# One shared pool of four PSUM banks for scores, transpositions and value products

## The chip, the cores and the metric

The kernel runs on one core of one Trainium2 chip. The metric is the device time of one execution in microseconds (us). The runs shown of the kernel before took 1342.78, 1343.08 and 1343.51 us; their median is 1343.08 us.

## The reference, cut to what matters

Two decoder layers over 512 tokens of width 1024: a recurrent layer (RG-LRU and SSD mixers), a SwiGLU FFN, a layer of dilated sliding-window attention with 16 heads of 64, and a second FFN. The change touches the attention layer, and the recurrent layer through the same pool of banks.

```python
s = jnp.einsum('bnqhe,bnkhe->bnhqk', qb, kc)
s = jnp.where(valid[None, :, None], s, -jnp.inf)
m = jnp.max(s, axis=-1)
p = jnp.exp(s - m[..., None])
o = jnp.einsum('bnhqk,bnkhe->bnqhe', p, vc)
```

The three (window, dilation) patterns are merged by their denominators. The kernel does that with one mask: it adds the logarithm of how many patterns allow a pair of tokens to its score, and takes a single softmax.

## The kernel before, in words

Everything stands transposed (channels on partitions, tokens along the free side). Each large product is made of three matmuls of split operands (high times high and the two mixed terms); the weights are loaded by SP, their high part is made by ACT and their low part by DVE (POOL for the attention's weights), line 107. PE is fed by these.

PSUM has eight banks, and a tile of 128 x 512 float32 fills one. Pool `pa` has four (tag `pa`: the projections, lines 234, 302, 735, 876). Pool `pm` has three under tag `pm` (`bufs=3`, line 77) and a fourth under tag `po` (line 848), which only the value product uses. Tag `pm` serves the sums of the norms (lines 212, 222), the recurrent layer (lines 319 to 554) and, in the attention:

- `pair_T(p)` (line 783): two tiles, the transposed queries and keys of a pair of heads; ACT and DVE copy them out as `qk_hi` and `qk_lo`.
- `scores(p)` (line 812): for both heads of a pair and three blocks b = 0, 1, 2 of query tiles, one tile per head (six tiles, called s0a, s0b, s1a, s1b, s2a, s2b below). DVE reads each piece once (line 833, mask and row minimum), ACT takes the exponential (line 834), DVE the reciprocal (line 837), POOL multiplies by it (line 839).
- `values(h)` (line 841): for each of three groups of key tiles, PE transposes the probabilities into a `pm` tile (line 855; 4, 4 and 2 transpositions), ACT and DVE split it (`ph`, `pl`, lines 91 and 92), and PE multiplies with the values into the one tile `ps_o` (lines 863, 864). Then ACT copies half of `ps_o` (line 866) and DVE adds the halves (line 867).

`attend(half)` (line 890) writes down: `pair_T` and `scores` of the next pair, then `values` of both heads of this one. The heads come in two halves of four pairs. The three parts of `qkv_part(1, ...)`, the projections of the second half, stand in the text behind the whole of `attend(0)`, and the output projection `out_proj(0, ...)` is called between the values of `attend(1)`.

The text isn't the order in which an engine works. When the kernel is built, the framework writes each engine's queue with a planner of its own: an instruction whose inputs are ready may be put ahead of earlier text, and a tile gets a bank of its tag when one comes free. On the chip each queue then runs in the order written, each instruction waiting for the semaphores of those it needs.

Of the kernel before, what the change touches and what calls it, by code (L numbers as in the profile page):

```python
# [10 lines left out]
F32 = mybir.dt.float32  # L11
# [6 lines left out]
P = 128  # L18
D = 1024
T = 512  # L20
# [39 lines left out]
def trunk(ctx: ExitStack, tc: tile.TileContext, a):  # L60
# [13 lines left out]
    ss_ = ctx.enter_context(tc.tile_pool(name="ss", bufs=2))  # L74
    fill(ss_, 320)
    pa = ctx.enter_context(tc.tile_pool(name="pa", bufs=4, space=bass.MemoryType.PSUM))
    pm = ctx.enter_context(tc.tile_pool(name="pm", bufs=3, space=bass.MemoryType.PSUM))


    specs = []  # L80
# [9 lines left out]
    def split(src, hi, lo, eng=V):  # L90
        S.copy(hi, src)  # L91
        eng.tensor_tensor(out=lo, in0=src, in1=hi.bitcast(F32), op=ALU.subtract)  # L92
# [83 lines left out]
    def slot(i, dtype):  # L176
        return [xp.tile([P, T], dtype, tag=f"x{z}{i}", name=f"x{z}{i}") for z in "hl"]
# [511 lines left out]
    with ExitStack() as actx:  # L689
# [151 lines left out]
        def values(h):  # L841
            p, e = h // 2, h % 2
            pr = prob.pop(h)
            rows = slice(64 * e, 64 * e + 64)
            if e == 0:
                o_of[p] = (at.tile([P, T], F32, tag="o", name="o", bufs=1), sp.tile([P, T], F32, tag="nsq", name="bot"))
            o, bot = o_of[p]
            po = pm.tile([P, T], F32, tag="po", name="ps_o", bufs=1)
            first = True
            for b in range(3):  # L850
                ps = pm.tile([P, T], F32, tag="pm", name="ps_pT")
                js = [(j, c) for j, (bj, c) in P_AT.items() if bj == b]
                for j, c in js:
                    for i in range(j, NT):
                        nc.tensor.transpose(ps[:, c + (i - j) * P:c + (i - j + 1) * P], pr[i][:, j * P:(j + 1) * P], ident)  # L855
                nb = 2 if b == 2 else 1
                hi = at.tile([P, WID[b]], F32R, tag=f"ph{b}", name="ph", bufs=nb)
                lo = at.tile([P, WID[b]], F32R, tag=f"pl{b}", name="pl", bufs=nb)
                split(ps[:, :WID[b]], hi, lo)
                for j, c in js:  # L860
                    n = T - j * P
                    v = vt[p // 4, j][:, h % 8].rearrange("p a e -> p (a e)")
                    mm(po[:, j * P:], lhsT=v, rhs=lo[:, c:c + n], start=first, stop=False)  # L863
                    mm(po[:, j * P:], lhsT=v, rhs=hi[:, c:c + n], start=False, stop=(b == 2))  # L864
                    first = False
            S.copy(bot[rows], po[64:])
            V.tensor_tensor(out=o[rows], in0=po[:64], in1=bot[rows], op=ALU.add)
            if e == 1:
                hi, lo = slot(8 + p if p < 4 else p - 4, F32R)
                split(o, hi, lo)  # L870
                oT.append((hi, lo))
# [18 lines left out]
        def attend(half, between):  # L890
            first = 4 * half
            pair_T(first)
            scores(first)
            for p in range(first, first + 4):
                if p < first + 3:
                    pair_T(p + 1)
                    scores(p + 1)
                for h in (2 * p, 2 * p + 1):
                    values(h)
                    for st in between.get(h, ()):  # L900
                        st()
# [102 lines left out]
```

## Time and profile before

| | us |
|---|---|
| median of the runs shown | 1343.08 |
| profiled execution, its own time | 1341.48 |
| its span, first to last instruction | 1339.7 |
| PE busy in it | 1315.5 |
| attention with pairs in flight, in the span | 783 to 956 |

The profiled execution took 1341.48 us, 1.78 us more than its span. All durations here are of this execution. The granted clock was 1.00 (2.4 GHz) in nearly all stretches; its mean is 0.997.

### The profile page before, as it was taken

Reading aid. Unit: us, or ns where it says so; the run is one execution under the profiler, and the core shown is the slowest. Engines: PE = TensorE matmul, PEld = TensorE weight load, DVE = VectorE, ACT = ScalarE, POOL = GpSimd, SP = SyncE. Lnnn points to the kernel's source line nnn. Section 1 sums busy time; section 2 is a strip of 40 time slices with the busy share of each in tenths; the row PEclk is TensorE's granted clock in tenths of the full one; section 3 lists DMA queues with packets and bytes.
Section 4 is the critical chain, followed back from the end, with each engine's and each line's share of the span. In section 5 each row is a group of like instructions: output and inputs, shape, how many; then the busy total and the mean of one; then the engine's idle time right before and its main releaser. Section 6 shows DMA issues by size and latency. Waiting matters only on the chain.

```text
span 1339.7 us, 15598 instructions
## 1 busy us (share of the span) xinstructions
PE 1315.5 (98%) x6122; PEld 1074.5 (80%) x6122; DVE 772.9 (58%) x1232; ACT 550.4 (41%) x810; POOL 120.3 (9%) x110
## 2 busy tenths in 40 slices
PE   8999989999999999999999999999999999999998
PEld 6877767788888888888888877877888888888887
DVE  7887799975544434434454666777754434444442
ACT  6743867443333222222333467546643212222321
POOL 0000000000000000000004453354200000000000
PEclk9999989999999999999999999999999999999999
DMA  6322222533232333332232321221133333333232
GB/s 240 111 86 87 95 79 71 174 102 95 94 95 94 95 95 95 91 108 99 89 101 95 95 79 33 63 79 48 41 102 94 95 95 98 99 87 110 95 93 80
DMA packets 38554, 126.51 MB, mean 94 GB/s; under 512 B 4288, under 2 KB 5056, under 8 KB 38352
## 3 DMA queue, kind: packets, MB, share of 16 engines
q1 hardware_dynamic: 38480, 125.51, 29.9%
q8 instruction: 48, 0.79, 0.2%
q14 instruction: 26, 0.21, 0.1%
HBM read 123.36 MB, written 2.13 MB: 94 GB/s over the span
## 4 chain that ended last, share of the span: by engine, by line
PE 92%; ACT 4%; DVE 3%; issue 1%; DMA 0%; SPq 0%; POOL 0%; DVEq 0%
PE ps_pr L114 24%; PE ps_pr L115 24%; PE ps_pr L116 24%; PE ps_qkv L743 3%; PE ps_qkv L744 3%; PE ps_qkv L745 3%; PE ps_pT L855 1%; ACT s L834 1%; PE ps_ao L116 1%; PE ps_ao L114 1%; PE ps_ao L115 1%; PE ps_s L826 1%; PE ps_o L863 1%; PE ps_o L864 1%; DVE s L833 1%
## 5 line engine op out<-in xcount | busy, mean ns | idle before, releaser
L91 ACT CAST wh<-wr 128x1024 fp32r<-128x1024 f32 (+2 forms) x223 | 228.4, 1025 | 641.1 <-PE ps_pr L116 379.7
L114 PE MATMUL ps_pr<-xh,wl 128*128 128x512 f32 x1056 | 416.4, 394 | 12.7 <-DVE wl L92 12.0
L115 PE MATMUL ps_pr<-xl,wh 128*128 128x512 f32 x1056 | 413.9, 392 | 0.0
L116 PE MATMUL ps_pr<-xh,wh 128*128 128x512 f32 x1056 | 413.0, 391 | 0.0
L92 DVE TENSOR_TENSOR wl<-wr,wh 128x1024 fp32r<-128x1024 f32 (+2 forms) x191 | 225.7, 1183 | 53.3 <-ACT wh L91 52.9
L114 PEld LDWEIGHTS ps_pr<-xh,wl 128*128 128x128 f32 x1056 | 199.3, 189 | 55.3 <-DVE wl L92 12.8
L115 PEld LDWEIGHTS ps_pr<-xl,wh 128*128 128x128 f32 x1056 | 199.4, 189 | 42.3 <-issue 1.1
L116 PEld LDWEIGHTS ps_pr<-xh,wh 128*128 128x128 f32 x1056 | 199.1, 189 | 42.2 <-issue 0.7
L114 PE MATMUL ps_pr<-ah,wl 128*128 128x512 f32 x352 | 136.9, 389 | 0.0
L115 PE MATMUL ps_pr<-al,wh 128*128 128x512 f32 x352 | 136.9, 389 | 0.0
L116 PE MATMUL ps_pr<-ah,wh 128*128 128x512 f32 x352 | 136.9, 389 | 0.0
L92 POOL TENSOR_TENSOR wl<-wr,wh 128x1024 fp32r<-128x1024 f32 x32 | 78.0, 2437 | 453.9 <-ACT wh L91 453.9
L671 DVE TENSOR_TENSOR tu<-ps_pr,nrb 128x512 f32<-128x512 f32 x44 | 30.4, 691 | 130.7 <-PE ps_pr L116 130.7
L679 DVE TENSOR_TENSOR x<-ps_pr,x 128x512 f32<-128x512 f32 x48 | 33.2, 692 | 120.4 <-PE ps_pr L116 120.3
L669 DVE TENSOR_TENSOR tg<-ps_pr,nrb 128x512 f32<-128x512 f32 x44 | 30.4, 691 | 93.7 <-PE ps_pr L116 93.7
L115 PEld LDWEIGHTS ps_pr<-al,wh 128*128 128x128 f32 x352 | 66.1, 188 | 13.8
L116 PEld LDWEIGHTS ps_pr<-ah,wh 128*128 128x128 f32 x352 | 66.1, 188 | 13.7
L114 PEld LDWEIGHTS ps_pr<-ah,wl 128*128 128x128 f32 x352 | 66.1, 188 | 13.7
L745 PE MATMUL ps_qkv<-wh,xh 128*128 128x512 f32 x192 | 75.5, 393 | 0.0
L743 PE MATMUL ps_qkv<-wh,xl 128*128 128x512 f32 x192 | 75.3, 392 | 0.0
L744 PE MATMUL ps_qkv<-wl,xh 128*128 128x512 f32 x192 | 75.3, 392 | 0.0
L744 PEld LDWEIGHTS ps_qkv<-wl,xh 128*128 128x128 f32 x192 | 36.1, 188 | 7.5
(234 smaller groups left out, 1494.7 us busy)
## 6 DMA issues: line engine op xcount, KB each, us to landing
wr<-in_w_gu SPq DMA_DIRECT2D x88, 512.0 KB, 3.5
wr<-in_w_in SPq DMA_DIRECT2D x35, 512.0 KB, 3.6
wr<-in_w_dn SPq DMA_DIRECT2D x32, 448.0 KB, 3.3
wr<-in_w_qkv SPq DMA_DIRECT2D x24, 512.0 KB, 3.5
wr<-in_w_out SPq DMA_DIRECT2D x16, 512.0 KB, 3.5
wr<-in_w_dn SPq DMA_DIRECT2D x16, 512.0 KB, 3.5
x<-in_xT SPq DMA_DIRECT2D x16, 256.0 KB, 3.6
bcs<-csd SPq DMA_DIRECT2D x16, 256.0 KB, 4.6
```

Of the source, the lines that this page charges most:

```text
L91: S.copy(hi, src)
L92: eng.tensor_tensor(out=lo, in0=src, in1=hi.bitcast(F32), op=ALU.subtract)
L114: mm(ps, lhsT=wl[ws], rhs=xh[xs], start=start, stop=False)
L115: mm(ps, lhsT=wh[ws], rhs=xl[xs], start=False, stop=False)
L116: mm(ps, lhsT=wh[ws], rhs=xh[xs], start=False, stop=stop)
L669: V.tensor_tensor(out=tg, in0=pg, in1=rb, op=ALU.mult)
L671: V.tensor_tensor(out=tu, in0=pu, in1=rb, op=ALU.mult)
L679: V.tensor_tensor(out=x[m], in0=ps, in1=x[m], op=ALU.add)
L743: mm(pss[t], lhsT=xl[:, ts_], rhs=wh[:, cols], start=(k == 0), stop=False)
L744: mm(pss[t], lhsT=xh[:, ts_], rhs=wl[:, cols], start=False, stop=False)
L745: mm(pss[t], lhsT=xh[:, ts_], rhs=wh[:, cols], start=False, stop=(k == KD - 1))
L826: mm(pss[e][:, c:c + n], lhsT=ql_[rows, qs], rhs=kr[rows, :n], start=(z == 0), stop=(z == 2))
```

## The change

The pool's tag `pm` gets four banks, and the value product takes one of these instead of a bank of its own. The number of banks in use stays eight. Arithmetic and instructions stay the same.

```diff
-    pm = ctx.enter_context(tc.tile_pool(name="pm", bufs=3, space=bass.MemoryType.PSUM))
+    pm = ctx.enter_context(tc.tile_pool(name="pm", bufs=4, space=bass.MemoryType.PSUM))
...
-            po = pm.tile([P, T], F32, tag="po", name="ps_o", bufs=1)
+            po = pm.tile([P, T], F32, tag="pm", name="ps_o")
```

## Rows read from the trace of the kernel before

**Rows 1.** The page: busy time, share of the span, instructions.
```profile
PE 1315.5 (98%) x6122; PEld 1074.5 (80%) x6122; DVE 772.9 (58%) x1232; ACT 550.4 (41%) x810; POOL 120.3 (9%) x110
```

**Rows 2.** Windows, the attention: us; busy time (instructions) of each engine; clock, DMA.
```profile
783.00:960.00 177.00, 169.68 (x962) 137.37 (x961) 120.85 (x302) 112.17 (x255) 73.90 (x81) 1.00 0.17 54
```

**Rows 3.** Waits of PE, whole span: us in total, times, longest.
```profile
PE ps_pr L114 <- DVE wl L92: 12.0, 3, 5.9
PE ps_s L826 <- DVE m L833: 7.0, 14, 0.8
```

**Rows 4.** Waits of PE, the first half's values (783 to 860).
```profile
PE ps_s L826 <- DVE m L833: 3.1, 6, 0.8
```

**Rows 5.** Timeline of PE, pair 5's scores, pair 4's values: start, length, what.
```profile
902.07 0.49 PE L826 MATMUL ps_s<-qk_lo,qk_hi 64*128 64x512 f32 x2
...
903.94 0.46 PE L826 MATMUL ps_s<-qk_lo,qk_hi 64*128 64x128 f32 x2 [0.62 <-DVE m L833]
...
906.64 0.39 PE L826 MATMUL ps_s<-qk_lo,qk_hi 64*128 64x256 f32 x1 [0.35 <-DVE m L833]
...
907.21 1.30 PE L855 MATMUL ps_pT<-cst,s 128*128 128x128 f32 x10
908.26 0.48 PE L115 MATMUL ps_ao<-xl,wh 128*128 128x512 f32 x1
...
910.24 0.50 PE L863 MATMUL ps_o<-pl,v 128*128 128x512 f32 x1
...
910.81 0.38 PE L855 MATMUL ps_pT<-cst,s 128*128 128x128 f32 x2
910.95 0.42 PE L863 MATMUL ps_o<-pl,v 128*128 128x384 f32 x1
```

**Rows 6.** Timeline of DVE in the same scores.
```profile
903.80 0.69 DVE L833 CUSTOM_DVE_ANT_0 s<-ps_s,cst 128x512 f32<-128x512 f32 x1
...
905.47 0.17 DVE L837 RECIPROCAL m<-m 128x2 f32<-128x2 f32 x1 [0.98 <-ACT s L834]
...
906.02 0.55 DVE L833 CUSTOM_DVE_ANT_0 s<-ps_s,cst 128x384 f32<-128x384 f32 x1
```

**Rows 7.** Groups by shape, ACT, 783 to 960: busy us, mean ns | idle before.
```profile
L91 ACT CAST ph<-ps_pT 128x512 fp32r<-128x512 f32 x32 | 17.0, 583 | 0.2
...
L834 ACT ACTIVATE s<-s,m 128x128 f32<-128x128 f32 x16 | 6.3, 394 | 2.9 <-DVE m L833 2.9
```

**Rows 8.** Groups by shape, DVE, 783 to 960.
```profile
L92 DVE TENSOR_TENSOR pl<-ps_pT,ph 128x512 fp32r<-128x512 f32 x32 | 20.6, 686 | 1.6 <-ACT ph L91 1.5
```

**Rows 9.** Timeline of POOL: the last six pieces of pair 1's probabilities.
```profile
801.96 2.75 POOL L839 TENSOR_SCALAR s<-s,m 128x128 f32<-128x128 f32 x6 [1.15 <-DVE m L837]
```

**Rows 10.** Timeline of DVE: the last splits of head 1's transpositions.
```profile
806.91 1.62 DVE L92 TENSOR_TENSOR pl<-ps_pT,ph 128x512 fp32r<-128x512 f32 x3
```

**Rows 11.** Timeline of PE: first and last of ten projections, then pair 1's transpositions.
```profile
809.85 0.48 PE L744 MATMUL ps_qkv<-wl,xh 128*128 128x512 f32 x1
...
812.01 0.39 PE L744 MATMUL ps_qkv<-wl,xh 128*128 128x512 f32 x1
...
817.46 1.29 PE L855 MATMUL ps_pT<-cst,s 128*128 128x128 f32 x10
```

**Rows 12.** Windows, instructions on ps_qkv alone, behind the first half's values.
```profile
852.00:889.60 37.60, 37.60 (x167) 30.97 (x165) 1.84 (x3) 4.83 (x7) 1.00 0.29 87
```

**Rows 13.** Windows, instructions on ps_ao alone, behind the last value product.
```profile
956.40:974.60 18.20, 18.16 (x80) 14.72 (x80) 3.84 (x6) 1.00 0.22 64
```

**Rows 14.** Timeline of PE: first and last of ten matmuls before the last split arrives.
```profile
956.44 0.40 PE L115 MATMUL ps_ao<-xl,wh 128*128 128x512 f32 x1
...
958.51 0.39 PE L115 MATMUL ps_ao<-xl,wh 128*128 128x512 f32 x1
```

**Rows 15.** Waits of PE's weight loads, recurrent layer.
```profile
PEld ps_yd L553 <- ACT ti L493: 1.5, 2, 0.8
```

**Rows 16.** Timeline of PE, recurrent layer, a projection behind those matmuls.
```profile
228.44 0.50 PE L114 MATMUL ps_pr<-xh,wl 128*128 128x512 f32 x1 [1.49 <-DVE wl L92]
```

## The prediction, made before the changed kernel was seen

> **What bounds the kernel.** I read the page's busy shares first: PE is busy 1315.5 of 1339.7 us [rows 1]. All its idle time is 24 us, so the change can gain no more than a part of that, and matmuls that are only moved cost nothing. The windows come next: in the attention, 783 to 960, PE idles 177 - 169.7 = 7.3 us [rows 2]. The waits of PE say on what: 7.0 us in 14 waits of the scores for DVE's reading of an earlier score tile [rows 3], that is, for a bank of tag `pm`. Of these 3.1 us lie in the first half's values [rows 4], so 3.9 in the second's. The other large wait, 12.0 us for split weights [rows 3], has nothing to do with banks.
>
> The timeline shows where the 14 waits stand. With three banks, s1b needs the bank of s0a and waits 0.62 us for its reading; s2b needs that of s1a and waits 0.35 [rows 5]. But the scores are part of a longer chain, which also runs through DVE and ACT. From s0's first matmul at 902.07 to pair 4's first value product at 910.24 it takes 8.2 us [rows 5], and the matmuls in it are short: ten transpositions need 1.05 us (907.21 to 908.26), then projections of the output stand in the queue to fill the time. The planner has put work there that doesn't depend on the values. This **fill** decides what a longer chain costs. In the first half it can't run out: 167 projections, 37.6 us, still stand behind its values [rows 12]. In the second half it is finite: 80 output matmuls stand behind the last value product [rows 13]. Sixty of them need the last pair's output (twelve closing terms of four open sums, 4 x 3, and 48 for the four outputs without a bank); of the others, ten run from 956.44 to 958.51 while the last split is made [rows 14]. Those ten, at 0.23 us each 2.3 us, are all the fill to spare, if as many are still needed there as ran.
>
> **Do banks follow the text?** This settles what a fourth shared bank does. Pair 1's last probabilities were multiplied by 804.71 [rows 9], and the last bank of head 1's transpositions was free by 808.53 [rows 10]. Yet PE ran ten projections from 809.85, which stand behind in the text, and transposed pair 1 only at 817.46, behind the scores of pair 2 [rows 11]. Ready inputs and a free bank were not enough: within a tag the tiles take banks in the order of the text, by first use, while work of other tags passes. So a shared tag gives a bank and also adds an order.
>
> **Part 1, scores.** s1b no longer needs s0a's bank, s2a takes s0a's and s2b takes s0b's, both read long before. All 14 waits should go. In the first half PE is the bound (projections cover the rest), so 3.1 us are gained: -3.1, between -3.1 and 0, since a queue written anew may wait elsewhere. In the second half the chain sets the end, and it isn't PE's: DVE and ACT take as long as before, and PE reaches the next transpositions earlier, only to wait or use more fill. I take 0, between -3.9 and 0.
>
> One piece of the chain does shrink. DVE read both s0 tiles by 904.49, waited 0.98 us in its reciprocal for ACT, and only behind it read s1 [rows 6]. With s1b done 0.6 us earlier, the planner may put s1's reading ahead of the reciprocal; then ACT loses its wait ahead of the 128 x 128 exponentials, 2.9 us over all pairs [rows 7]. Half of that lies in the second half: -1.5, between -1.5 and 0. In the first half it shortens only a covered chain.
>
> **Part 2, values.** First uses within a value become pT0, ps_o, pT1, pT2, because ps_o is first written by the first product. Before, all ten transpositions preceded the first product, their splits running meanwhile, and the second group of products followed at 910.95 [rows 5]. Now the second transpositions must follow the first product: its group ends at 910.81, four transpositions take 0.42 (10 in 1.05) and some 0.3 until their result is seen (the last product's length, 0.38, less its slot), `ph` takes 0.58 [rows 7] and `pl` 0.69 [rows 8]. 910.81 + 0.42 + 0.3 + 0.58 + 0.69 = 912.80, so 1.85 us later per value. In the first half projections hide it. In the second half a head's delay is in the chain only where no other head's tiles are ahead: the second head's pT0 may be transposed as soon as the first head's pT0 is split, so I count the end of pairs 5 and 6 and the end of the half, three groups: 3 x 1.85 = 5.5, less the 2.3 us of spare fill, +3.2. Bounds: 0 (first products have a split ready in all eight values), and all eight, 14.8 - 2.3 = +12.5.
>
> The Trainium skill ("PSUM — Partial Sum Buffer", § Engine vs sequencer instructions) says that matmuls start and complete in program order; by that rule a delayed transposition holds up every matmul queued behind it. The bounds would be the same by it.
>
> **Part 3, the rest.** ps_o's bank is freed by lines 866 and 867. pair_T's second tile takes it, one pair's end later, with fill or other heads' work in between: 0, at most one copy and one addition of about the split's 0.58 and 0.69, inside the bounds above. In the recurrent layer a fourth bank may end the waits of line 553 for `ti`, 1.5 us in two [rows 15]; but a projection behind them already waits 1.49 us for split weights [rows 16], and PE arriving earlier waits longer there. I take 0, between -1.5 and +4.0: the upper end is one more weight wait, 12.0 / 3 [rows 3], since the order of ACT and DVE is written anew too. The norms' sums are short and alone: 0. No DMA, no POOL or SP work is added; POOL's multiplications move with the probabilities and are covered by the same fill.
>
> **The sum.** -3.1 + 0 - 1.5 + 3.2 + 0 = -1.4 us against the profiled 1341.48: 1340.1. The median of the runs is 1.60 us above the profiled one, so **1341.7 us** as a median. A measurement of this kernel can tell about 0.2%, 2.7 us, from no change: the forecast is no change.
>
> **Rivals.**
> A, faster: the 14 waits go in both halves and the order costs nothing, because first products are always ready before the second transpositions would have mattered. -7.0: 1336.1. For it: the waits are nearly all that PE idles in the attention (7.0 of 7.3). Against it: the chain of DVE and ACT stays as long. The Trainium skill ("Perfetto Trace Analysis", § Optimization Strategy) takes the same gap repeated on the engine that should be full as a sign that the next tile has no buffer; by that rule A is right. The trace agrees on the sign (14 equal waits), and can't show that the gaps don't come back elsewhere.
>
> B, slower: the order within a value delays all eight values of the second half. It happens between ps_o's first product and pT1, costs 1.85 us each, and decides once the 2.3 us of spare fill are used, after the second value: 14.8 - 2.3 - 3.1 = +9.4, 1352.5. For it: each value's transpositions were prefetched before its first product [rows 5]. Against it: half of the heads have a neighbour whose tiles go ahead.
>
> C, the change does nothing: one value uses four tiles of the tag, ps_o falls on the same bank each time, the three others rotate as before, and the queue hardly changes: 1343.1. Against it: the scores see four banks, whatever the values do.
>
> **How the numbers follow.** The forecast's case has 0.43, with a range of its own of 1338.5 to 1345.5 (its first term lost, or the scores' 3.9 gained in part); A 0.27, B 0.22, C 0.08. The range reaches to A and its -1.5 of ACT, 1335, and to B, 1352.5. Faster by over 2.7 us, below 1340.4: A's 0.25 and 0.11 of the forecast's; slower, above 1345.8: B's 0.20 and 0.04 of the forecast's; the rest, 0.40, is no change.
>
> **What would show it.** Part 1 is right if the waits of the scores for `m` fall from 7.0 to near 0, and wrong if others of PE (transpositions or products waiting for `s` or `pl`) take their place in the first half too. The ACT term is right if its 2.9 us ahead of the 128 x 128 exponentials fall. Part 2 is right if in PE's timeline the second transpositions stand behind the first product, with products waiting for `pl` or more fill between them; the number of output matmuls behind the last value product then falls from 80 to 70 or below, and under 70 PE must idle. If all ten transpositions still precede the first product, part 2 and B are wrong. If the line 553 waits go and the weight waits stay at 12.0, part 3 is right. A queue in which other tags' matmuls have moved by many microseconds, with waits that stand in none of these rows, would make the whole sum wrong.

## The result, and the profile after

| | before | after |
|---|---|---|
| median of the runs, us | 1342.93 | 1350.96 (1350.83 to 1351.23) |
| profiled execution / its span, us | 1341.48 / 1339.7 | 1351.0 / 1349.2 |
| PE busy / idle in the span, us | 1315.5 / 24.2 | 1320.1 / 29.1 |

The changed kernel is 8.0 us slower, a ratio of 1.0057 with an interval of 1.0045 to 1.0069. The forecast was 1341.7 us, no change. The page of the changed kernel splits the 9.5 us of span without a remainder: PE idles 4.9 us more and is busy 4.6 us longer with the same 6122 instructions [rows 1].

```profile
PE 1320.1 (98%) x6122; PEld 1075.3 (80%) x6122; DVE 775.1 (57%) x1232; ACT 556.3 (41%) x813; POOL 120.4 (9%) x110
```

The idle part is read from PE's waits in the changed kernel (us in total, times, longest), to be held against [rows 3].

```profile
PE ps_pr L114 <- DVE wl L92: 11.5, 3, 5.9
PE ps_pT L855 <- DVE m L833: 6.0, 6, 1.6
PE ps_pT L855 <- DVE o L867: 2.0, 1, 2.0
PE ps_s L826 <- DVE m L833: 1.8, 8, 0.2
PE ps_ao L114 <- ACT xh L91: 1.1, 1, 1.1
PE ps_pr L115 <- DVE xl L192: 0.9, 1, 0.9
PE ps_qT L788 <- DVE m L833: 0.8, 1, 0.8
```

The scores' waits fell from 7.0 to 1.8 us: eight of 0.23 us are left of fourteen. But 6.0 us of waiting for the same reads (`m`, line 833) now stand ahead of the transpositions of a value, and 0.8 ahead of pair_T: 8.6 us in place of 7.0. Beside them there are three waits of 0.9 us or more that the kernel before did not have: for line 867, for the last split (`xh`), and for the first input of the FFN (`xl`).

Where such a wait stands is seen in PE's timeline of the changed kernel, second pair (start, length, what).

```profile
797.65 0.38 PE L826 MATMUL ps_s<-qk_lo,qk_hi 64*128 64x256 f32 x1 [0.23 <-DVE m L833]
...
798.20 0.50 PE L744 MATMUL ps_qkv<-wl,xh 128*128 128x512 f32 x1
798.54 0.39 PE L745 MATMUL ps_qkv<-wh,xh 128*128 128x512 f32 x1
799.78 0.63 PE L855 MATMUL ps_pT<-cst,s 128*128 128x128 f32 x4 [0.84 <-DVE m L833]
...
803.45 0.40 PE L863 MATMUL ps_o<-pl,v 128*128 128x512 f32 x1
803.68 0.39 PE L864 MATMUL ps_o<-ph,v 128*128 128x512 f32 x1
803.91 1.25 PE L855 MATMUL ps_pT<-cst,s 128*128 128x128 f32 x10
```

The scores run nearly without a stop, two projections follow, and then PE stands 0.84 us for the bank of pT0. Behind the four transpositions of pT0 comes the first product, and only behind that ten more transpositions (4 + 2 of this head, 4 of the next): the order that the shared tag was expected to force. DVE's timeline of the same scores says why the bank is late: a tag's banks are taken in turn, in a ring, so with four of them pT0 takes the bank of s1a.

```profile
796.29 0.69 DVE L833 CUSTOM_DVE_ANT_0 s<-ps_s,cst 128x512 f32<-128x512 f32 x1 [1.55 <-PE ps_s L826]
...
798.58 0.17 DVE L837 RECIPROCAL m<-m 128x2 f32<-128x2 f32 x1 [0.98 <-ACT s L834]
798.66 0.27 DVE L833 CUSTOM_DVE_ANT_0 s<-ps_s,cst 128x128 f32<-128x128 f32 x1
...
799.07 0.55 DVE L833 CUSTOM_DVE_ANT_0 s<-ps_s,cst 128x384 f32<-128x384 f32 x1
```

PE has finished s1 by then (its last matmul starts at 796.78), but DVE still waits 0.98 us in the reciprocal before it reads s1, as in [rows 6]. s1a's second piece is read until 799.62 (799.07 + 0.55), and pT0 starts 0.16 us later. From s0's first read to s1's first read it takes 798.66 - 796.29 = 2.37 us. In the kernel before, the same two reads of this pair are as far apart:

```profile
796.89 0.69 DVE L833 CUSTOM_DVE_ANT_0 s<-ps_s,cst 128x512 f32<-128x512 f32 x1 [2.27 <-PE ps_s L826]
...
799.26 0.27 DVE L833 CUSTOM_DVE_ANT_0 s<-ps_s,cst 128x128 f32<-128x128 f32 x1
```

PE got its bank earlier, and the engine that empties the banks did not get faster.

The busy part is the clock. Windows of the changed kernel (us; length; busy time and count of PE, PEld, DVE, ACT, POOL; granted clock, DMA share, GB/s):

```profile
834.00:840.00 6.00, 4.26 (x17) 3.24 (x18) 5.60 (x28) 4.57 (x17) 4.23 (x7) 0.76 0.29 90
840.00:846.00 6.00, 6.00 (x34) 5.15 (x32) 5.93 (x13) 2.10 (x4) 1.38 (x3) 0.96 0.00 0
846.00:858.00 12.00, 10.00 (x54) 8.51 (x54) 9.23 (x13) 5.33 (x11) 2.40 (x1) 0.86 0.14 44
...
912.00:918.00 6.00, 6.00 (x24) 4.78 (x23) 2.10 (x8) 2.27 (x9) 2.78 (x6) 0.72 0.15 58
```

In the kernel before, the clock is 1.00 over the attention [rows 2]. Here TensorE falls to its lower level (1.2 GHz) three times: behind the longest wait of a transposition (1.60 us, to 837.02), behind the wait for line 867 (2.00 us, to 850.09), and behind a wait of 0.90 us at 911.55. Matmuls of 512 columns then start 0.43 us apart in place of 0.23:

```profile
837.02 1.04 PE L855 MATMUL ps_pT<-cst,s 128*128 128x128 f32 x4 [1.60 <-DVE m L833]
...
838.29 0.63 PE L743 MATMUL ps_qkv<-wh,xl 128*128 128x512 f32 x1
838.72 0.63 PE L744 MATMUL ps_qkv<-wl,xh 128*128 128x512 f32 x1
```

One minus the clock, times the length, summed over these rows, is 1.44 + 0.24 + 1.68 + 1.68 = 5.0 us, near the 4.6 that PE is busy longer (in part of these stretches PE idled, so the sum comes out somewhat high).

The order's own cost shows in the fill. Windows of the changed kernel, of the projections behind the first half's values and of the output matmuls behind the last value product:

```profile
861.10:895.00 33.90, 33.61 (x149) 27.49 (x147) 2.25 (x3) 5.08 (x8) 1.00 0.27 84
```

```profile
967.05:990.00 22.95, 15.02 (x64) 11.77 (x64) 5.04 (x8) 1.00 0.27 79
```

The values used 18 projections more than before in the first half (167 to 149 [rows 12]) and 16 output matmuls more in the second (80 to 64 [rows 13]). The ten spare ones and six more were gone when the last split was due: the waits of 1.1 and 0.9 us are the part that found no cover.

What the order does to one value is seen at the last one: the first matmul of its first and of its second group of products, in the changed kernel and then in the kernel before.

```profile
963.57 0.50 PE L863 MATMUL ps_o<-pl,v 128*128 128x512 f32 x1
...
966.19 0.40 PE L863 MATMUL ps_o<-pl,v 128*128 128x384 f32 x1
```

```profile
954.84 0.50 PE L863 MATMUL ps_o<-pl,v 128*128 128x512 f32 x1
...
955.63 0.33 PE L863 MATMUL ps_o<-pl,v 128*128 128x384 f32 x1
```

The second group stands 2.62 us behind the first, before 0.79: 1.83 us later. But the first products of the last four heads follow each other 3.5 to 4.1 us apart, before 3.7 to 4.1, so not every head pays this.

### The profile page after: what moved, and what is told of

Read it like the earlier page. It is cut to its first block, busy times and chain, and to the rows that moved or that the text cites. A ratio compares the mean times of both kernels' runs of the same rounds, so it can differ in the third digit from the quotient of the medians.

```text
span 1349.2 us, 15601 instructions
## 1 busy us (share of the span) xinstructions
PE 1320.1 (98%) x6122; PEld 1075.3 (80%) x6122; DVE 775.1 (57%) x1232; ACT 556.3 (41%) x813; POOL 120.4 (9%) x110
## 4 chain that ended last, share of the span: by engine, by line
PE 91%; DVE 5%; ACT 3%; issue 1%; DMA 0%; SPq 0%; POOL 0%; DVEq 0%
PE ps_pr L114 24%; PE ps_pr L115 24%; PE ps_pr L116 24%; PE ps_qkv L743 3%; PE ps_qkv L744 3%; PE ps_qkv L745 3%; ACT s L834 1%; PE ps_pT L855 1%; PE ps_o L863 1%; PE ps_ao L114 1%; DVE s L833 1%; PE ps_ao L116 1%; PE ps_ao L115 1%; PE ps_o L864 1%; PE ps_yd L553 1%
## 5 line engine op out<-in xcount | busy, mean ns | idle before, releaser
L114 PE MATMUL ps_pr<-xh,wl 128*128 128x512 f32 x1056 | 416.5, 395 | 11.8 <-DVE wl L92 11.5
L116 PEld LDWEIGHTS ps_pr<-ah,wh 128*128 128x128 f32 x352 | 66.1, 188 | 13.7
L743 PEld LDWEIGHTS ps_qkv<-wh,xl 128*128 128x128 f32 x192 | 36.5, 190 | 7.4
```

The costliest lines, as they stand in the source:

```text
L114: mm(ps, lhsT=wl[ws], rhs=xh[xs], start=start, stop=False)
L116: mm(ps, lhsT=wh[ws], rhs=xh[xs], start=False, stop=stop)
L743: mm(pss[t], lhsT=xl[:, ts_], rhs=wh[:, cols], start=(k == 0), stop=False)
```

## The experiments

Two theories. **O**: the shared tag's order costs the time, because the second transpositions stand behind the first product. **W**: the fourth bank lets PE reach pT0 before DVE has read s1; the waits move there, and the clock falls behind them.

**Three banks, shared.** ps_o stays in the tag, and the tag gets three banks again.

```diff
-    pm = ctx.enter_context(tc.tile_pool(name="pm", bufs=4, space=bass.MemoryType.PSUM))
+    pm = ctx.enter_context(tc.tile_pool(name="pm", bufs=3, space=bass.MemoryType.PSUM))
```

> The value product shares the tag as in the change, but the tag keeps three banks (seven in use). Theory O (the shared order costs the time: the second transpositions stand behind the first product): as slow as the change or slower, 1351 to 1360, with no wait of ps_pT for line 867 needed to explain it. Theory W (the fourth bank costs it, because PE now reaches the first transposition before DVE has read s1 and idles there about 1 us per pair, and TensorE's clock falls behind such a wait): the waits of the scores stay at about 7.0 us as before, ps_pT waits for DVE's m stay under 2, and the time is near the kernel before, 1343 to 1347.

Measured 1368.51 us, ratio 1.0187 (1.0163 to 1.021). Waits of PE in it:

```profile
PE ps_s L826 <- DVE m L833: 8.4, 13, 2.9
PE ps_o L863 <- DVE pl L92: 6.1, 6, 1.6
PE ps_ao L114 <- ACT xh L91: 4.8, 3, 2.0
```

Sharing without a new bank costs 25.9 us, more than theory O had it: products wait for splits (6.1) and the fill ends early (4.8; 60 output matmuls are left behind the last value product). PE idles 13.7 us more than in the kernel before and is busy 15.9 us longer, at a lower clock (mean 0.986 in place of 0.997). This run has the shared order and one bank less in all (seven), and doesn't tell the two apart; with the fourth bank 17.6 of the 25.9 us are given back. W does not explain this kernel, but neither is W refuted: no fourth bank, no wait of pT0.

**All transpositions first.** The change, with the text of `values` in two loops, so that ps_o is the last of a value's four tiles to be written.

```diff
+            parts = []
...
                 split(ps[:, :WID[b]], hi, lo)
+                parts.append((b, js, hi, lo))
+            for b, js, hi, lo in parts:
                 for j, c in js:
```

> The change, and in values() all three tiles are transposed and split in the text before the first product, so ps_o comes last of a value's four tiles. Theory O: the cost goes, at most the 1343 of the kernel before, perhaps 1340 if the scores' waits are really gained. Theory W: the waits of ps_pT for DVE's m stay at 6 us, the clock in 783 to 960 still falls below 1.00 in places, and the time stays at 1348 to 1351.

Measured 1346.18 us, ratio 1.0025 (1.0016 to 1.0034): 4.8 us less than the change, so that much of the loss is the order's, and 3.6 us above the kernel before as it ran beside this one (1342.59). Both theories are right in part. PE's waits in it, and behind them the window of one of its two stretches with a lower clock:

```profile
PE ps_pT L856 <- DVE m L833: 4.4, 5, 0.9
PE ps_s L826 <- DVE m L833: 2.5, 9, 0.7
PE ps_o L866 <- DVE pl L92: 2.4, 1, 2.4
```

```profile
816.00:822.00 6.00, 5.56 (x23) 4.83 (x24) 3.42 (x13) 3.91 (x15) 3.55 (x8) 0.72 0.00 0
```

The waits for line 867, for `xh` and for the FFN's `xl` are gone, 2.0 + 1.1 + 0.9 = 4.0 us, and 80 output matmuls stand behind the last value product again. That isn't the 4.8 us itself: another wait, 2.4 us for `pl`, is new, and in the profiled executions PE idles only 1.8 us less than in the change and is busy 3.4 us less. What W predicted stays in part: 4.4 us ahead of the transpositions, and stretches with a lower clock.

**One reciprocal per pair, on the kernel before.** All eight row sums of a pair go through one reciprocal behind the last read, so no read can stand behind a wait for the exponentials.

```diff
+            m = am.tile([P, 3, 8], F32, tag="m", name="m", bufs=6)
+            done = []
...
-                V.reciprocal(m[:, 2, :len(done)], m[:, 1, :len(done)])
...
+            V.reciprocal(m[:, 2], m[:, 1])
```

> The kernel before with one reciprocal for all three blocks of a pair, behind all of DVE's score reads, so that no read stands behind DVE's wait of 0.98 us for the exponentials. If that wait is what the 14 score waits are made of: they fall from 7.0 to under 4 us and the time to 1339 to 1342. If the banks alone make them: 7.0 us stay and 1343.

Measured 1342.67 us, ratio 0.9999 (0.9989 to 1.0008): nothing. The scores' waits fell, to 5.0 us in 8, and a wait of 2.2 us for `pl` is new. DVE's timeline shows what came in the reciprocal's place with three banks:

```profile
812.99 0.69 DVE L833 CUSTOM_DVE_ANT_0 s<-ps_s,cst 128x512 f32<-128x512 f32 x1 [0.74 <-PE ps_s L828]
...
814.85 0.29 DVE L833 CUSTOM_DVE_ANT_0 s<-ps_s,cst 128x128 f32<-128x128 f32 x1 [0.55 <-PE ps_s L828]
```

The reads are 1.86 us apart in place of 2.41: now DVE waits 0.55 us for PE, which had waited 0.62 us for s0a's bank. With three banks each side waits for the other in turn.

**One reciprocal per pair, on the change.** The same edit.

> The same single reciprocal on the change. Theory W: DVE has read s1 about 0.9 us earlier, so the 6.0 us of ps_pT waits for m fall to under 2, the clock stays at 1.00 behind them, and the time is 1343 to 1346. Theory O: the second transpositions still stand behind the first product, 1349 to 1351.

Measured 1342.98 us, ratio 1.0001 (0.9991 to 1.0011): all 8.0 us are back, with the order as the change has it. In the profiled executions PE idles 4.2 us less than in the change and is busy 4.0 us less. PE's waits, and then from the timeline of the second pair DVE's two reads, the first transpositions and POOL's multiplications:

```profile
PE ps_s L828 <- DVE m L833: 1.8, 8, 0.2
PE ps_pT L855 <- DVE m L833: 1.6, 1, 1.6
PE ps_pT L855 <- DVE o L867: 1.3, 1, 1.3
PE ps_ao L114 <- ACT xh L91: 1.1, 1, 1.1
```

```profile
796.41 0.69 DVE L833 CUSTOM_DVE_ANT_0 s<-ps_s,cst 128x512 f32<-128x512 f32 x1 [1.54 <-PE ps_s L828]
...
797.64 0.28 DVE L833 CUSTOM_DVE_ANT_0 s<-ps_s,cst 128x128 f32<-128x128 f32 x1
...
798.90 0.60 PE L855 MATMUL ps_pT<-cst,s 128*128 128x128 f32 x4
...
801.96 2.63 POOL L839 TENSOR_SCALAR s<-s,m 128x512 f32<-128x512 f32 x5 [2.31 <-DVE m L837]
```

s1 is read 1.23 us behind s0, pT0 starts without a wait, and five of the six waits of a transposition for `m` are gone; the mean clock from 783 to 975 is 1.00. The POOL row excludes another reading. In the change, the waits of these transpositions' weight loads, 8.5 us in six, are put down to POOL's multiplications (line 839), which ran at about the same time. Here those, of the next pair's probabilities, start 3 us later than the transposition, so it doesn't wait for them.

**Both edits.** Transpositions first and one reciprocal, on the change.

> Both edits on the change: all three tiles transposed before the first product, and one reciprocal per pair. Two-cause theory (the order cost 4.8 us and the late reading of s1 behind the reciprocal cost 8.0, partly the same time, since each alone gave that back): with neither, the fourth bank's gain is left, 1338 to 1342, waits of ps_pT for m under 2 us. Rival (the shared tag costs in any order, since ps_o and the next tiles queue for one ring): 1343 to 1346 as with the transpositions first alone.

Measured 1339.55 us, ratio 0.9976 (0.9965 to 0.9986): faster than both kernels, and 3.4 us faster than the kernel before as it ran beside it (1342.96). The rival, that a shared tag costs in any order, falls. Where the 3.4 us lie the profile doesn't show: the profiled execution took 1341.23 us, the slowest of the eight and nearly that of the kernel before (1341.48). Its waits:

```profile
PE ps_o L866 <- DVE pl L92: 4.1, 6, 2.2
PE ps_s L828 <- DVE m L833: 2.5, 9, 0.6
PE ps_pT L856 <- DVE m L833: 0.3, 1, 0.3
```

The four cases with four banks now form a square (medians in us, of runs beside which the kernel before took 1342.6 to 1343.0):

| | three reciprocals | one reciprocal |
|---|---|---|
| product before the second transpositions | 1350.96 | 1342.98 |
| all transpositions first | 1346.18 | 1339.55 |

The order costs 4.8 or 3.4 us, the late reading 8.0 or 6.6, nearly independent of each other. Held against three banks with one reciprocal (1342.67), the shared pool of four is 3.1 us faster, where DVE empties the banks in time and all transpositions come first. The transpositions-first text was not run with three banks beside ps_o's own, so these 3.1 us are not shown to be the bank's alone.

**ACT empties ps_o alone.** The change, with the wait for line 867 taken from DVE's queue.

```diff
-            V.tensor_tensor(out=o[rows], in0=po[:64], in1=bot[rows], op=ALU.add)
+            S.copy(o[rows], po[:64])
+            V.tensor_tensor(out=o[rows], in0=o[rows], in1=bot[rows], op=ALU.add)
```

> The change, and ACT copies both halves of ps_o, DVE adds from SBUF. The 2.0 us wait of ps_pT for line 867 (whose DVE queue held 2.9 us of rotary products) goes. If that wait and the clock behind it count in full: 3 us less than the change, 1348. If projections cover it, since it lies in the first half where time is PE's: it still is PE idle, so at least 2 us less; ACT's 16 more copies of 0.58 us lie in the chain at the values and may give back up to 16 x 0.58 / 2 = 4.6 us: 1348 to 1353.

Measured 1359.79 us, ratio 1.0124 (1.0109 to 1.014): a miss. That wait is gone, but products now wait for their splits:

```profile
PE ps_pT L855 <- DVE m L833: 6.5, 6, 2.1
PE ps_o L863 <- DVE pl L92: 4.1, 4, 1.8
PE ps_ao L114 <- ACT xh L91: 1.5, 1, 1.5
```

The loss of 8.8 us against the change is near the length of the added copies, 16 x 0.58 = 9.3 us, of which half was expected; but the profile doesn't show them as lost one by one. PE idles 4.4 us more than in the change, and it is busy 4.3 us longer: half of the loss is the clock again. That the copies lengthen the chain to `pl` fits the new waits and is not shown step by step.

**Two tiles first, the third behind the first products.** The change, with the first tile's products held back until the second tile is transposed and split.

```diff
+            parts = []
...
                 split(ps[:, :WID[b]], hi, lo)
+                parts.append((b, js, hi, lo))
+                if b == 0:
+                    continue
+                for b_, js, hi, lo in parts:
...
+                parts = []
```

> The change with two tiles transposed before the first product, the third behind it: half of the order's cost by its own place. If each transposition behind the first product costs alike: between the change and the version with all first, 1348 to 1350. If only the long second tile counts (the third takes 0.38 us of ACT and less of DVE): 1346 to 1348. Output matmuls behind the last value product between 64 and 80.

Measured 1346.49 us, ratio 1.0027 (1.0016 to 1.0038), no different from all transpositions first. So the second tile, with its 0.58 and 0.69 us of splitting, is worth being ahead; that the short third one is too, these runs don't show.

**One reciprocal, and ACT empties ps_o.** Both of these edits on the change.

> The change with one reciprocal per pair and ACT copying both halves of ps_o. Without the 1.3 us wait for line 867 that the one-reciprocal version still had: 1341 to 1342.5; if ACT's added copies lengthen the chain: 1343 to 1347.

Measured 1352.98 us, ratio 1.0066 (1.0054 to 1.0079), 10.0 us above one reciprocal alone and far above the 1347 that was expected at most: ACT's copies cost about as much here as above (8.8), so their cost hardly depends on the reciprocal's place. In the profiled executions (1351.25 and 1342.78) PE idles 4.2 us more and is busy 4.2 us longer.

## Why the prediction was wrong

**The step that failed is part 1, the scores**, in the sentence "In the first half PE is the bound ...: -3.1, between -3.1 and 0". The scores' waits did fall (7.0 to 1.8; the rest is ahead of s2b, since s0b, "read long before" in the prediction, was being read until 797.59 when PE came to it at 797.42). But 6.8 us of waits for the same reads came back, most of them one tile later. In the first half the scores' waits went from 3.1 to 0.9 us, and 3.3 came in ahead of pT0 (0.84, 0.90 and 1.60): +1.2 in place of -3.1. The prediction had said for the second half that PE "reaches the next transpositions earlier, only to wait or use more fill", which is what happened, and it did not apply this to the first half. There fill was plentiful, yet PE takes its queue in order: two projections stood ahead of pT0, and the next ones ran only behind it, though the 0.84 us would have held three more. Plenty of fill behind a wait covers nothing. Both halves together gave +1.6 and not -3.1.

**The clock was missing from the sum.** Moved waits come in other lengths. Before, there were eight of 0.5 to 0.8 us and six of 0.3; after, beside the eight of 0.23, seven of 0.8 to 1.6 and one of 2.0. Three times TensorE fell to its lower level behind one, and PE was busy 4.6 us longer. No row of the kernel before showed a lower clock in the attention, and the prediction took a moved wait to cost only its own length.

**The ACT term (-1.5) failed too.** The planner kept the reciprocal ahead of s1's reads though s1 was ready, so the reads did not move (2.37 us in both). The term's own sign, ACT's idle time ahead of the 128 x 128 exponentials, rose from 2.9 to 4.0 us. The experiments show that the term had the right place, and that it needed an edit of its own: with s1 read early this idle time is 1.2 us. The 8.0 us that came back with it are PE's waits and the clock, which the term did not count.

**Part 2 was right in its mechanism.** Second transpositions stand behind the first product, and at the last value this costs 1.83 us where 1.85 was worked out (the 0.38 that went into it as a product's length is that of two transpositions in [rows 5], without harm to the sum); output matmuls behind the last product fell to 64 (70 or below was expected, and under 70 PE must idle, as it does). The forecast was +3.2; the idle time at the end is 1.1 + 0.9 = 2.0, and undoing the order gave 4.8. Another part of that is the wait for line 867: the prediction took that for 0 (part 3), with pair_T's second tile as the one to wait. It was a transposition of a head, for 2.0 us in the first half, because DVE had 2.9 us of the second half's rotary products queued ahead of the addition. Part 3's 0 was right for the recurrent layer, though not by its reason: the 1.5 us for `ti`, which a fourth bank was thought to end, stand as before; the weight waits are 11.5 against 12.0, and the first scores start 0.1 us from where they did.

**The rivals.** B gave 1352.5 and the sign, and it named the right order, but not where most of the time went: eight values paying 1.85 us each isn't what the trace has (the heads follow each other as fast as before), undoing the order returns 4.8 us and undoing the late reading returns 8.0. That its number is so near is luck, and so is it that the measured time lies inside the stated range, at the end that B had set. A comes near only after DVE's queue and the order of the transpositions are put right, and then the gain is 3.1 to 3.4 us, not 7.0. The sign that A drew from the Trainium skill ("Perfetto Trace Analysis", § Optimization Strategy), equal gaps as a possible want of buffers, held for the place of the gaps; that a buffer by itself removes them, as A took it, the trace does not bear out, since 7.0 us of gaps became 8.6. With the rule of the Trainium skill on program order ("PSUM — Partial Sum Buffer", § Engine vs sequencer instructions) the trace agrees: no matmul ran in the waits of pT0, and all that stood behind it in PE's queue waited with it, 6.0 us in all.

What stays open is which of these waits makes the clock fall. In the changed kernel it fell behind 0.90 us at 911.55, but not behind 0.90 us at 817.36, and with one reciprocal not behind waits of 1.6 and 1.3 us. These runs don't tell it apart.

## What to carry to other kernels

Before giving a waiting engine one more buffer, follow the buffer to the engine that empties it, and ask in which order that engine's queue does so: here DVE's reads stood behind a reciprocal that waited for ACT, and the new bank only moved the wait to the next tile of the ring. A ring shared by tiles of different stages also orders these stages, so write the tiles in the text in the order in which they should run (here all long transpositions before the first product). And fill counts as cover only if it stands ahead of the waiting instruction in the queue.

## What the runs showed that was not expected

Sharing a tag of three banks among the value product and the rest cost 25.9 us, though it takes away no more than one bank of eight. Two changes that are each worth nothing or a loss (one reciprocal with three banks: 0.9999; four shared banks: 1.0057) are together level, and with a third edit faster than the kernel before (0.9976). And in the changed kernel PE lost nearly as much behind its waits as in them: 4.6 us more busy, with a clock of 0.72 to 0.96 in four stretches, beside 4.9 us more idle. The experiments that lost most show the same pairing: 15.9 busy beside 13.7 idle with three shared banks (against the kernel before), 4.3 beside 4.4 with ACT's copies (against the change).
